# A hybrid encoder block: the last additions of v as accumulating stores, and the small work of q and k in groups of four

## The chip, the cores and the metric

The kernel runs on one core of one Trainium2 chip. The metric is device microseconds for one execution of the whole program; lower is better. The core has a matrix engine (PE), a vector engine (DVE), a scalar engine (ACT) and a general engine (POOL); SP only issues DMAs here. Each engine takes its instructions strictly in its own program order, and semaphores hold an instruction until what it reads is there and what it overwrites has been read. Times inside the execution are counted from the start of the profiled span.

## The reference

The input has 512 tokens of 1024 channels. One normalised input feeds three token mixers (a pooling mixer, a linear recurrence and an attention) and their gates; the outputs are merged and projected, and a SwiGLU network follows. What the change touches is this, cut from the reference:

```python
# linear recurrence (width 1024)
log_a = (-LRU_C * r) * softplus(-lru_lambda)
a = exp(log_a)
b = sqrt(-expm1(2.0 * log_a)) * (i * xc)
_, h = lax.associative_scan(combine, (a, b), axis=1)      # h[s] = a[s] * h[s-1] + b[s]

# attention: q, k, v are 512 x 1024 each, cut from h @ w_in, as 8 heads of 128
q = rms_norm(q, q_norm)        # over the 128 channels of a head
k = rms_norm(k, k_norm)
y = stick_breaking_attention(q, k, v)
```

So q and k need, per token and head, the sum of 128 squares and a scaling by its inverse root; v is used as the projection leaves it.

## The kernel before

**Matmuls in three passes.** Every large product in float32 is done as three passes of a rounded type: high part of the data by high part of the weight, high by low, low by high. `split_w` (L134 to L143) makes the parts of each weight tile of 128x1024: ACT copies the raw tile into `whi` (L141), DVE subtracts it from the raw tile into `wlo` (L142). In the program order of PE the second matmul of a tile is the first that reads `wlo`. The tiles come from a pool with three buffers of each kind, so the parts of one tile may be written once PE is through with the tile three places earlier.

**Products of v, k and q.** The three projections run one after the other in the order v, k, q (t = 2, 1, 0). Each is a two by two block product done with seven products instead of eight (`ORDER`: 11, 12, S2, S1, S3, S4, 22), and each of the seven is two weight tiles of 12 matmuls (`tok_product`, L836). The weights of S2, S1, S3 and S4 are sums of the four loaded blocks: `qs` (L214) and the second form of `qw` (L209) are such sums on DVE, and others are built by DMAs that add while they load (POOL, L200 and L215). This text numbers the tiles as the program does: `wlo24` to `wlo37` belong to v, 38 to 51 to k, 52 to 65 to q. A *block* is one tile's 12 matmuls.

**Quarters of the result.** Each projection has four quarters, (0,0), (0,1), (1,0), (1,1). A quarter is the sum of two PSUM tiles that are ready at different times: `snap` copies the first to SBUF as `r` (ACT, L857), and `final` adds the second to it (DVE, L865, 128x1024). For v, `post` then stores `r` to `qd` in DRAM (POOL, L790). For k it takes squares with row sums (ACT, eight small instructions, L803), forms the inverse root on POOL and DVE, scales (ACT, eight small instructions, L823), transposes (DVE, L814) and stores; for q the scaling is applied later.

**The recurrence runs beside v.** Its four channel chunks end in passes of DVE over 128x1024: `lru_decay` (L703), `lru_input` (L711 and L712), two scans of 128x512 (`lru_scan`, L717), then `lru_store`, which copies to a high part `yh` on ACT (L722), subtracts on DVE (L723) and stores both (POOL, L725). Chunks 2 and 3 are still open when v begins.

**What sets the order.** Small pieces of work lie in a list, `bg`, and `tick()` takes one from it, once before and once after the matmuls of each tile. Above that a scheduler of the build sorts by priority: `high_priority` moves an instruction ahead, and `issue_after(x)` keeps instructions behind x in the order. `issue_after` decides the order alone and adds no wait on the chip. All weight loads are issued on SP's queue; adding loads and stores lie on POOL's.

Of the kernel before, what the change touches and what calls it, by code (L numbers as in the profile page):

```python
# [64 lines left out]
def layer_kernel(ctx: ExitStack, tc: tile.TileContext, x, xt, vecs, w_in, w_qkv7, w_gate7, w_pool, w_rg, w_ig,  # L65
# [65 lines left out]

    los, raws = [], []

    def split_w(raw, shape, n):  # L134
        hi, lo = weight_tiles("whi" + n, "wlo" + n)
        if len(shape) == 3:
            hi, lo = (t.rearrange("p (a b) -> p a b", a=shape[1]) for t in (hi, lo))
        else:
            hi, lo = (t.rearrange("p (a b c) -> p a b c", a=shape[1], b=shape[2]) for t in (hi, lo))
        with tc.high_priority(60):  # L140
            act(hi, raw, AF.Copy)  # L141
            los.append(dve.tensor_tensor(lo, raw, hi.bitcast(F32), ALU.subtract).ins)  # L142
        return hi, lo  # L143
# [47 lines left out]
    def seven_load(n, nms):  # L191
# [3 lines left out]
        for nm in nms:  # L195
            for i in range(pieces):
                qraw[u, nm, i] = r = b4(list(shape), f"qw{u}{nm}{i}", "w")
                nc.sync.dma_start(r, seven_src(u, nm, i))
                if nm == "21":
                    nc.gpsimd.dma_start(r, seven_src(u, "22", i), accum_op=ALU.add)  # L200

    def add_seven(un, nm, i):
        u, pieces, shape = UNITS[un]
        last = i == pieces - 1

        def make(n):
            if nm == "S4":
                r = qraw[u, "12", i]
                dve.tensor_tensor(r, r, qraw[u, "S2", i], ALU.add)  # L209
            src = qraw[u, {"S1": "21", "S3": "11", "S4": "12"}.get(nm, nm), i]  # L210
            parts = split_w(src, [P] + list(shape), n)
            if nm == "11":
                qraw[u, "S2", i] = r = b4(list(shape), f"qs{u}{i}")
                dve.tensor_tensor(r, qraw[u, "21", i], src, ALU.add)  # L214
                add = nc.gpsimd.dma_start(src, seven_src(u, "21", i), accum_op=ALU.add)  # L215
            if last:
# [220 lines left out]
    with ExitStack() as first:  # L437
# [322 lines left out]
        def of(f, c):  # L760
            return lambda: f(c)
# [17 lines left out]
        gate1(2)  # L779
        for f, c in ((lru_decay, 2), (lru_decay, 3), (lru_input, 2)):  # L780
            step(of(f, c))
# [11 lines left out]
        def post(t, i, j, r):  # L793
            if t == 2:
                store(t, i, j, r)
                return
            z = b4([2, 512], f"sq{t}{i}{j}")
            sums = qss[:, 2 * j:2 * j + 2, 4 * i:4 * i + 4] if t == 0 else cst.tile(
                [P, 2, 4], F32, tag="ssq", name=f"ssq{t}{i}{j}", bufs=2)
            for a in range(2):  # L800
                for n in range(4):
                    cs = slice(n * HD, (n + 1) * HD)
                    act(z[:, a, cs], r[:, a, cs], AF.Square, accum_out=sums[:, a, n:n + 1])  # L803
            if t == 0 and i > j:
                state["last"] = lambda: turn(t, i, j, r, z)
                return
            if t == 0:
                turn(t, i, j, r, z)
                return
            dve.tensor_scalar(sums, sums, 1.0 / HD, EPS, ALU.mult, ALU.add)  # L810
            bg.append(lambda: post2(t, i, j, r, z, sums))

# [4 lines left out]
        def post2(t, i, j, r, z, s_):  # L817
            y = cst.tile([P, 2, 4], F32, tag="krs", name=f"krs{i}{j}", bufs=2)
            rsqrt(y, s_, (2, 4), f"q{t}{i}{j}")
            for a in range(2):  # L820
                for n in range(4):
                    v = r[:, a, n * HD:(n + 1) * HD]
                    act(v, v, AF.Copy, scale=y[:, a, n:n + 1])  # L823
            turn(t, i, j, r, z)

# [23 lines left out]
        for t in VKQ:  # L849
# [4 lines left out]
            def snap(key, src):  # L854
                r[key] = b4([2, 512], f"r{t}{key[0]}{key[1]}")
                with tc.high_priority(EARLY):
                    state["snap"] = act(two(r[key]), in_order(src), AF.Copy, scale=-1.0 if key[0] else 1.0)  # L857
# [5 lines left out]
            def final(key, src):  # L863
                v = two(r[key])
                dve.tensor_tensor(v, v, in_order(src), ALU.subtract if key[0] else ALU.add)  # L865
# [9 lines left out]
            for nm in ORDER:  # L875
# [928 lines left out]
```

## Time and profile before

| | |
|---|---|
| three runs, median | 860.64 us (859.68 to 860.79) |
| the profiled execution | 858.89 us |
| its span, first to last instruction | 856.8 us |
| PE busy | 850.3 us (99% of the span) |
| DVE, ACT, POOL busy | 732.3, 533.3, 88.6 us |
| granted TensorE clock | 1.00 throughout |

The gates before v end near 138 us of the span; v takes the stretch from there to about 176 us, k to about 213, and q to about 249. In the groups and timelines, `out<-in` gives the tiles that an instruction writes and reads, and the bracket at the end of a row tells how long the engine stood still before it, and what ended that. Matmuls overlap in the pipeline, so their rows of 0.38 us start 0.216 us apart when nothing is waited for, and a larger step between two starts is a stall.

### The profile page before, as it was taken

How to read it: one execution, taken by the hardware profiler on the slowest of the kernel's cores; microseconds unless marked ns; L12 is line 12 of the kernel's file. 1: busy time of each engine (PE TensorE's matmuls, PEld its weight loads, DVE VectorE, ACT ScalarE, POOL GpSimd, SP SyncE). 2: the span in 40 equal slices, each digit the busy share in tenths (PEclk: the TensorE clock that was granted, in tenths of full speed). 3: DMA queues.
4: the chain of work that ended last, by engine and by line, in shares of the span. 5: the costliest groups of instructions: out<-in, count | busy, mean ns of one | idle time of the engine just before them, and what ended most of it. 6: DMA issues, size and time to landing. Idle time of an engine off the chain costs nothing.

```text
span 856.8 us, 14307 instructions
## 1 busy us (share of the span) xinstructions
PE 850.3 (99%) x5483; PEld 781.2 (91%) x5483; DVE 732.3 (85%) x937; ACT 533.3 (62%) x863; POOL 88.6 (10%) x128
## 2 busy tenths in 40 slices
PE   9999999999999999999999999999999999999998
PEld 7888888888889988889889988889999999999998
DVE  7899898987897699967997877799988888999974
ACT  6554999658887657556665544455655555755642
POOL 1110002123324102000001100000000000121200
PEclk9999999999999999999999999999999999999999
DMA  9586356798585768846668854364533434797913
GB/s 343 160 286 205 101 167 200 215 316 262 141 257 129 228 170 239 246 116 171 174 204 212 182 197 148 99 164 136 145 99 109 114 101 142 221 238 204 199 32 123
DMA packets 141988, 154.09 MB, mean 180 GB/s; under 512 B 41696, under 2 KB 115424, under 8 KB 141920
## 3 DMA queue, kind: packets, MB, share of 16 engines
q1 hardware_dynamic: 129248, 107.30, 40.6%
q0 software_dynamic: 12528, 45.62, 22.5%
q8 instruction: 43, 0.70, 0.3%
q10 hardware_dynamic: 144, 0.26, 0.1%
q14 instruction: 25, 0.20, 0.1%
HBM read 132.71 MB, written 18.87 MB: 177 GB/s over the span
## 4 chain that ended last, share of the span: by engine, by line
PE 88%; ACT 4%; DVE 4%; issue 3%; POOL 1%; DMA 0%; DVEq 0%; POOLq 0%
PE ps_y L315 11%; PE ps_x L315 8%; PE ps_dy L1723 6%; PE ps_q L844 5%; PE ps_dx L1723 5%; PE ps_br L306 3%; PE ps_br L307 3%; PE ps_br L308 3%; PE ps_bY L1347 3%; PE ps_gy L315 3%; PE ps_gate L736 2%; PE ps_bX L1347 2%; PE ps_gx L315 2%; PE ps_pool L308 2%; PE ps_pool L306 2%
## 5 line engine op out<-in xcount | busy, mean ns | idle before, releaser
L141 ACT ACTIVATE whi<-raw 128x1024 fp32r<-128x1024 f32 x69 | 72.9, 1056 | 75.6 <-PE ps_br L307 18.4
L142 DVE TENSOR_TENSOR wlo<-raw,whi 128x1024 fp32r<-128x1024 f32 x69 | 84.2, 1220 | 22.4 <-ACT whi L141 21.9
L142 DVE TENSOR_TENSOR wlo<-qw,whi 128x1024 fp32r<-128x1024 f32 x48 | 58.3, 1220 | 11.6 <-ACT whi L141 11.2
L141 ACT ACTIVATE whi<-qw 128x1024 fp32r<-128x1024 f32 x48 | 50.4, 1052 | 23.6 <-PE ps_q L844 12.8
L1508 ACT ACTIVATE wh_S<-w_S 128x1024 fp32r<-128x1024 f32 x36 | 38.3, 1063 | 28.7 <-PE ps_y L315 20.0
L1629 POOL DMA_DIRECT2D dw<-in_w_down_dram x20 | 17.0, 855 | 305.3 <-DMA dw<-in_w_down_dram 247.7
L1509 DVE TENSOR_TENSOR wl_S<-w_S,wh_S 128x1024 fp32r<-128x1024 f32 x36 | 43.8, 1220 | 3.3 <-ACT wh_S L1508 3.3
L1508 ACT ACTIVATE wh<-w 128x1024 fp32r<-128x1024 f32 x27 | 28.6, 1061 | 28.0 <-PE ps_x L315 9.4
L1509 DVE TENSOR_TENSOR wl<-w,wh 128x1024 fp32r<-128x1024 f32 x27 | 32.9, 1220 | 8.2 <-ACT wh L1508 8.2
L1508 ACT ACTIVATE whdS<-dw 128x1024 fp32r<-128x1024 f32 x20 | 21.2, 1061 | 20.7 <-PE ps_dy L1723 10.6
L1155 DVE TENSOR_TENSOR_SCAN E<-K,ahead 128x512 f32<-128x512 f32 (+3 forms) x32 | 25.4, 814 | 4.6 <-ACT K L1151 4.6
L1509 DVE TENSOR_TENSOR wldS<-dw,whdS 128x1024 fp32r<-128x1024 f32 x20 | 24.3, 1221 | 5.2 <-ACT whdS L1508 5.2
L306 PE MATMUL ps_lru<-HH,whi 128*128 128x512 f32 x64 | 24.6, 384 | 0.0
L306 PE MATMUL ps_br<-yph,whi 128*128 128x512 f32 x64 | 24.4, 382 | 0.0
L306 PE MATMUL ps_gate<-HH,whi 128*128 128x512 f32 x64 | 24.4, 381 | 0.0
L307 PE MATMUL ps_br<-ypl,whi 128*128 128x512 f32 x64 | 24.3, 380 | 0.0
L306 PE MATMUL ps_pool<-HH,whi 128*128 128x512 f32 x64 | 24.3, 379 | 0.0
L306 PE MATMUL ps_br<-yHH,whi 128*128 128x512 f32 x64 | 24.3, 379 | 0.0
L307 PE MATMUL ps_lru<-HL,whi 128*128 128x512 f32 x64 | 24.3, 379 | 0.0
L308 PE MATMUL ps_lru<-HH,wlo 128*128 128x512 f32 x64 | 24.3, 379 | 0.0
L307 PE MATMUL ps_gate<-HL,whi 128*128 128x512 f32 x64 | 24.3, 379 | 0.0
L308 PE MATMUL ps_gate<-HH,wlo 128*128 128x512 f32 x64 | 24.3, 379 | 0.0
(742 smaller groups left out, 3432.1 us busy)
## 6 DMA issues: line engine op xcount, KB each, us to landing
raw<-in_w_in_dram SPq DMA_DIRECT2D x31, 512.0 KB, 5.1
qw<-in_w_qkv_dram SPq DMA_DIRECT2D x24, 512.0 KB, 7.2
dw<-in_w_down_dram POOLq DMA_DIRECT2D x20, 512.0 KB, 7.7
w<-in_w_ffn_gate_dram SPq DMA_DIRECT2D x36, 256.0 KB, 3.9
w<-in_w_ffn_up_dram SPq DMA_DIRECT2D x36, 256.0 KB, 4.1
raw<-in_w_branch_dram SPq DMA_DIRECT2D x16, 512.0 KB, 3.8
qw<-in_w_qkv_dram POOLq DMA_DIRECT2D x12, 512.0 KB, 7.6
g<-gd SPq DMA_DIRECT2D x24, 256.0 KB, 4.5
```

The costliest lines, as they stand in the source:

```text
L141: act(hi, raw, AF.Copy)
L142: los.append(dve.tensor_tensor(lo, raw, hi.bitcast(F32), ALU.subtract).ins)
L306: nc.tensor.matmul(ps, lh, rh, start=start, stop=False, skip_group_check=skip)
L307: nc.tensor.matmul(ps, lh, rl, start=False, stop=False, skip_group_check=skip)
L308: nc.tensor.matmul(ps, ll, rh, start=False, stop=stop, skip_group_check=skip)
L315: nc.tensor.matmul(o, a_[a][:, w, k, :], il2(b_[b][:, k, :]), start=first and n == k == 0, stop=last and n == 2 and k == 3, skip_group_che ...
L844: nc.tensor.matmul(ps[:, a, :], b_[:, k, ts_], il(a_[:, kk, :]), start=first and n == k == 0, stop=n == 2 and k == 3, skip_group_check=True)
L1155: dve.tensor_tensor_scan(E[:, c0:c0 + n][:, ::-1], K[:, c0 + 1:c0 + n + 1][:, ::-1], ahead[:, S - n:][:, ::-1], 0.0, ALU.mult, ALU.add)
L1347: nc.tensor.matmul(o, ah[x_][:, w, k, :], il2(b[k][y_]), start=first_ and n == k == 0, stop=n == 2 and k == 3, skip_group_check=True)
L1508: act(h, src, AF.Copy)
L1509: dve.tensor_tensor(l, src, h.bitcast(F32), ALU.subtract)
L1723: nc.tensor.matmul(o, a_[a][:, w, k0 + k, :], il2(b_[b][:, k, :]), start=first and i == k == 0, stop=last and i == 2 and k == nk - 1, skip ...
```

## The change

**v.** `snap` stores its copy `r` to `qd` at once. The second PSUM tile of a quarter is copied to SBUF by ACT (`add_store`, a tile `v`), and a DMA on POOL's queue with an adding write puts it on top of what is in `qd`. The four additions L865 of v leave DVE; four copies on ACT and four stores of 512 KB come in. An adding store waits for the landing of the plain store to the same rows.

**The recurrence.** The high part `yh` of chunks 0 and 1 is made on DVE instead of ACT, and the second half of `lru_decay` of chunks 2 and 3 too. The passes L711, L712 and L717 of chunks 2 and 3, the sums `qs` and the additions L209 of v's weights stand behind named low parts (`seven_lo`).

**q and k.** The eight squares and the eight scalings of a quarter are issued as two groups of four, each placed behind the newest `whi`, with two ticks between the groups.

Nothing is changed in the order of PE or of SP. DVE has one row fewer, ACT one fewer, POOL four more. Lines behind L199 move down by 7, those of the end by 34.

```diff
@@ split_w
-    los, raws = [], []
+    his, los, raws = [], [], []
...
-            act(hi, raw, AF.Copy)
+            his.append(act(hi, raw, AF.Copy).ins)
@@ add_seven
+    seven_lo = {}
...
-                dve.tensor_tensor(r, r, qraw[u, "S2", i], ALU.add)
+                with tc.issue_after(seven_lo["S2", i]) if un == 0 else nullcontext():
+                    dve.tensor_tensor(r, r, qraw[u, "S2", i], ALU.add)
...
-            if nm == "11":
+            if un == 0:
+                seven_lo[nm, i] = los[-1]
+            if nm == ("12" if un == 0 else "11"):
+                first_ = qraw[u, "11", i]
                 qraw[u, "S2", i] = r = b4(list(shape), f"qs{u}{i}")
-                dve.tensor_tensor(r, qraw[u, "21", i], src, ALU.add)
-                add = nc.gpsimd.dma_start(src, seven_src(u, "21", i), accum_op=ALU.add)
+                with tc.issue_after(los[-1]) if un == 0 else nullcontext():
+                    dve.tensor_tensor(r, qraw[u, "21", i], first_, ALU.add)
+                add = nc.gpsimd.dma_start(first_, seven_src(u, "21", i), accum_op=ALU.add)
@@ lru_decay, lru_store
-            if c < 2:
-                dve.tensor_scalar(t, t, -1.0, 1.0, ALU.mult, ALU.add)
-            else:
-                act(t, t, AF.Identity, scale=-1.0, bias=1.0)
+            dve.tensor_scalar(t, t, -1.0, 1.0, ALU.mult, ALU.add)
...
-            act(h, y, AF.Copy)
+            if c < 2:
+                dve.tensor_copy(h, y)
+            else:
+                act(h, y, AF.Copy)
@@ post (k, q)
-            for a in range(2):
-                for n in range(4):
-                    cs = slice(n * HD, (n + 1) * HD)
-                    act(z[:, a, cs], r[:, a, cs], AF.Square, accum_out=sums[:, a, n:n + 1])
+            def squares(a):
+                with nullcontext() if t == 0 and i > j else behind_hi():
+                    for n in range(4):
+                        cs = slice(n * HD, (n + 1) * HD)
+                        act(z[:, a, cs], r[:, a, cs], AF.Square, accum_out=sums[:, a, n:n + 1])
...
+            squares(0)
...
+                bg.extend([nothing, nothing, then])
+        def behind_hi():
+            return tc.issue_after(his[-1])
@@ post2 (k)
+            scale(0)
+            bg.extend([nothing, nothing, lambda: (scale(1), turn(t, i, j, r, z))])
@@ the loop over v, k, q
+                if t == 2:
+                    store(t, *key, r[key])
...
+            def add_store(key, src):
+                part = b4([2, 512], f"v{key[0]}{key[1]}")
+                with tc.high_priority(EARLY):
+                    act(two(part), in_order(src), AF.Copy, scale=-1.0 if key[0] else 1.0)
+                nc.gpsimd.dma_start(rows(t, *key), part, accum_op=ALU.add)
...
             def final(key, src):
+                if t == 2:
+                    add_store(key, src)
+                    return
...
+                if t == VKQ[0]:
+                    for f, after_ in {"11": ((lambda: lru_input(2), ("12", 0)), (lambda: lru_input(3), ("12", 1))),
+                                      "12": ((lambda: lru_scan(2, 0), ("S2", 0)), (lambda: lru_scan(2, 1), ("S2", 1))),
+                                      "S2": ((lambda: lru_scan(3, 0), ("S1", 0)), (lambda: lru_scan(3, 1), ("S1", 1)))
+                                      }.get(nm, ()):
+                        with tc.issue_after(seven_lo[after_]):
+                            f()
                 if (t, nm) == (VKQ[0], "S3"):
-                    def last_scan():
-                        for j in range(2):
-                            with tc.issue_after(los[j - 5]):
-                                lru_scan(3, j)
-
-                    step(of(lru_input, 3)), step(of(lru_scan, 2)), step(last_scan)
                     step(of(lru_store, 2)), step(of(lru_store, 3))
```

On DVE, at the start of v, the order before around the low parts of the third, fourth and fifth tile (`wlo_1341` is wlo26, `wlo_1368` is wlo27, `wlo_1395` is wlo28; `qs`, `qw` are sums of v's weights; `lt`, `ls`, `li` belong to the recurrence):

```order
L214 TENSOR_TENSOR qs_1262<-qw_1194,qw_1200 128x1024
L214 TENSOR_TENSOR qs_1302<-qw_1197,qw_1202 128x1024
L703 SCALAR_TENSOR_TENSOR lt_1224<-lr_1082,lt_1224 128x1024
L142 TENSOR_TENSOR wlo_1341<-qw_1204,whi_1340 128x1024
L711 SCALAR_TENSOR_TENSOR ls_1249<-lr_897,ls_1249 128x1024
L209 TENSOR_TENSOR qw_1204<-qw_1204,qs_1262 128x1024
L142 TENSOR_TENSOR wlo_1368<-qw_1206,whi_1367 128x1024
L712 TENSOR_TENSOR ls_1249<-ls_1249,li_898 128x1024
L142 TENSOR_TENSOR wlo_1395<-qs_1262,whi_1394 128x1024
```

and now, where `wlo_1333` is wlo26, `wlo_1363` wlo27 and `wlo_1398` wlo28:

```order
L142 TENSOR_TENSOR wlo_1294<-qw_1202,whi_1293 128x1024
L711 TENSOR_SCALAR lt_1118<-lt_1118 128x1024
L711 TENSOR_SCALAR lt_1224<-lt_1224 128x1024
L142 TENSOR_TENSOR wlo_1333<-qw_1204,whi_1332 128x1024
L221 TENSOR_TENSOR qs_1336<-qw_1194,qw_1200 128x1024
L715 SCALAR_TENSOR_TENSOR ls_1249<-lr_897,ls_1249 128x1024
L142 TENSOR_TENSOR wlo_1363<-qw_1206,whi_1362 128x1024
L221 TENSOR_TENSOR qs_1366<-qw_1197,qw_1202 128x1024
L142 TENSOR_TENSOR wlo_1398<-qs_1336,whi_1397 128x1024
```

The two sums `qs` stood ahead of wlo26, and now stand behind wlo26 and wlo27; the addition to `qw` and the pass L712 that stood around wlo27 have moved further back.

On DVE, later in v, the order before from wlo31 (`wlo_1445`) to wlo35 (`wlo_1526`):

```order
L142 TENSOR_TENSOR wlo_1445<-qw_1197,whi_1444 128x1024
L712 TENSOR_TENSOR ls_1251<-ls_1251,li_1083 128x1024
L717 SCALAR_TENSOR_TENSOR li_898<-lt_1118,ls_1249 128x512
L142 TENSOR_TENSOR wlo_1470<-qw_1200,whi_1469 128x1024
L142 TENSOR_TENSOR wlo_1486<-qw_1202,whi_1485 128x1024
L717 SCALAR_TENSOR_TENSOR li_1083<-lt_1224,ls_1251 128x512
L142 TENSOR_TENSOR wlo_1509<-qw_1204,whi_1508 128x1024
L717 SCALAR_TENSOR_TENSOR li_1083<-lt_1224,ls_1251 128x512
L142 TENSOR_TENSOR wlo_1526<-qw_1206,whi_1525 128x1024
```

and now, from wlo31 (`wlo_1451`) to wlo36 (`wlo_1562`):

```order
L142 TENSOR_TENSOR wlo_1451<-qw_1197,whi_1450 128x1024
L716 TENSOR_TENSOR ls_1251<-ls_1251,li_1083 128x1024
L721 SCALAR_TENSOR_TENSOR li_898<-lt_1118,ls_1249 128x512
L142 TENSOR_TENSOR wlo_1479<-qw_1200,whi_1478 128x1024
L721 SCALAR_TENSOR_TENSOR li_1083<-lt_1224,ls_1251 128x512 x2
L142 TENSOR_TENSOR wlo_1495<-qw_1202,whi_1494 128x1024
L142 TENSOR_TENSOR wlo_1519<-qw_1204,whi_1518 128x1024
L142 TENSOR_TENSOR wlo_1536<-qw_1206,whi_1535 128x1024
L142 TENSOR_TENSOR wlo_1562<-qw_1208,whi_1561 128x1024
```

wlo33 (`wlo_1486` before) stood right behind wlo32; now both scans of the last chunk (one row, x2) stand between wlo32 and wlo33 (`wlo_1495`), and none behind it.

On POOL, the DMAs from the middle of the gates' stores (`gd`) to the stores of the recurrence, before (`qd` are the results in DRAM, `qw` the adding loads; `qw_1448` and `qw_1451` are blocks 21 of k):

```order
L215 DMA qw_1200<-in_w_qkv_dram 128x1024
L215 DMA qw_1202<-in_w_qkv_dram 128x1024
L603 DMA gd_96<-gt_1253 128x2x512
L603 DMA gd_97<-gt_1335 128x2x512
L790 DMA qd_88<-r_1391 128x2x512
L200 DMA qw_1448<-in_w_qkv_dram 128x1024
L200 DMA qw_1451<-in_w_qkv_dram 128x1024
L790 DMA qd_89<-r_1505 128x2x512
L725 DMA ydh_103<-yh_1585 128x1024
L725 DMA ydl_105<-li_898 128x1024
```

and now, where `v` are the new adding stores and `qw_1454` and `qw_1457` the same blocks of k:

```order
L610 DMA gd_96<-gt_1253 128x2x512
L610 DMA gd_97<-gt_1327 128x2x512
L222 DMA qw_1200<-in_w_qkv_dram 128x1024
L222 DMA qw_1202<-in_w_qkv_dram 128x1024
L797 DMA qd_88<-r_1389 128x2x512
L891 DMA qd_88<-v_1429 128x2x512
L200 DMA qw_1454<-in_w_qkv_dram 128x1024
L797 DMA qd_88<-r_1472 128x2x512
L200 DMA qw_1457<-in_w_qkv_dram 128x1024
L797 DMA qd_89<-r_1514 128x2x512
L891 DMA qd_89<-v_1555 128x2x512
L797 DMA qd_89<-r_1558 128x2x512
```

The adding loads of v have gone behind the stores of gates, the adding store of (0,0) stands ahead of the first block of k, a plain store ahead of the second, and the adding store of (1,1) ahead of the store of (1,0) and of all that follows on the queue, the stores of chunks 2 and 3 of the recurrence first.

More of the change, by code (lines that the diff above doesn't have):

```diff
@@ L779, in layer_kernel @@
         gate1(2)
-        for f, c in ((lru_decay, 2), (lru_decay, 3), (lru_input, 2)):
+        for f, c in ((lru_decay, 2), (lru_decay, 3)):
             step(of(f, c))
@@ L793, in post @@
         def post(t, i, j, r):
-            if t == 2:
-                store(t, i, j, r)
-                return
             z = b4([2, 512], f"sq{t}{i}{j}")
@@ L799, in post, with then @@
                 [P, 2, 4], F32, tag="ssq", name=f"ssq{t}{i}{j}", bufs=2)
-            for a in range(2):
-                for n in range(4):
-                    cs = slice(n * HD, (n + 1) * HD)
-                    act(z[:, a, cs], r[:, a, cs], AF.Square, accum_out=sums[:, a, n:n + 1])
-            if t == 0 and i > j:
[L805 to L811, printed above, removed]
+            def squares(a):
[3 more added lines that the diff above has]
+                        act(z[:, a, cs], r[:, a, cs], AF.Square, accum_out=sums[:, a, n:n + 1])
+            def then():
+                squares(1)
+                if t == 0 and i > j:
+                    state["last"] = lambda: turn(t, i, j, r, z)
+                    return
+                if t == 0:
+                    turn(t, i, j, r, z)
+                    return
+                dve.tensor_scalar(sums, sums, 1.0 / HD, EPS, ALU.mult, ALU.add)
+                bg.append(lambda: post2(t, i, j, r, z, sums))
+            squares(0)
+            if t == 0 and i > j:
+                then()
+            else:
+                bg.extend([nothing, nothing, then])
+        def behind_hi():
+            return tc.issue_after(his[-1])
         def turn(t, i, j, r, z):
@@ L819, in post2, with scale @@
             rsqrt(y, s_, (2, 4), f"q{t}{i}{j}")
[L820 to L824, printed above, removed]
+            def scale(a):
+                with behind_hi():
+                    for n in range(4):
+                        v = r[:, a, n * HD:(n + 1) * HD]
+                        act(v, v, AF.Copy, scale=y[:, a, n:n + 1])
+            scale(0)
+            bg.extend([nothing, nothing, lambda: (scale(1), turn(t, i, j, r, z))])
         def q_scales():
```

1 line of the change is left out of this document (added).

## Prediction

> **What bounds the kernel now.** I read the page's first part, then the waits of PE, then the busy time by windows over v, k and q, then PE and DVE in order of time around each stall.
>
> ```profile
> span 856.8 us, 14307 instructions
> PE 850.3 (99%) x5483; PEld 781.2 (91%) x5483; DVE 732.3 (85%) x937; ACT 533.3 (62%) x863; POOL 88.6 (10%) x128
> ...
> PE ps_q L844 <- DVE wlo L142: 1.5, 4, 0.5
> PE ps_q0S L844 <- DVE wlo L142: 0.2, 1, 0.2
> ...
> 140.00:150.00 10.00, 9.16 (x41) 7.39 (x41) 10.00 (x10) 9.16 (x12) 3.27 (x4) 1.00 0.79 180
> 150.00:160.00 10.00, 10.00 (x48) 8.74 (x48) 10.00 (x10) 5.14 (x5) 1.45 (x2) 1.00 0.53 179
> 160.00:170.00 10.00, 9.64 (x45) 8.13 (x44) 9.10 (x9) 6.40 (x7) 1.88 (x4) 1.00 0.94 229
> 170.00:180.00 10.00, 10.00 (x48) 8.77 (x47) 10.00 (x10) 5.45 (x6) 4.64 (x7) 1.00 1.07 408
> 220.00:230.00 10.00, 9.71 (x45) 8.20 (x44) 8.87 (x10) 10.00 (x25) 1.20 (x2) 1.00 0.22 68
> 230.00:240.00 10.00, 9.78 (x45) 8.12 (x44) 6.00 (x9) 8.01 (x21) 3.71 (x4) 1.00 0.98 302
> ```
>
> PE is the bound. The change leaves PE's order alone, so it can only win what PE stands still in v, k and q, and by the two rows of waits that is 1.7 us, all of it for a `wlo` of DVE. The windows (columns: PE, PEld, DVE, ACT, POOL, clock, DMA share, GB/s) put it at 140 to 150, 160 to 170 and in q at 220 to 240; windows without a stall hold 10.00. The missing PE time of the four windows is 0.84 + 0.36 + 0.29 + 0.22 = 1.71 us. In v DVE is full (10.00), so there a low part is late because of what stands before it on DVE.
>
> The starts of the matmuls give the full price of a stall:
>
> ```profile
> 140.69 0.38 PE L844 MATMUL ps_q<-whi,HH 128*128 128x512 f32 x1
> 140.90 0.38 PE L844 MATMUL ps_q<-wlo,HH 128*128 128x512 f32 x1
> ...
> 143.28 0.38 PE L844 MATMUL ps_q<-whi,HH 128*128 128x512 f32 x1
> 143.95 0.48 PE L844 MATMUL ps_q<-wlo,HH 128*128 128x512 f32 x1 [0.29 <-DVE wlo L142]
> 144.27 0.38 PE L844 MATMUL ps_q<-whi,HL 128*128 128x512 f32 x1
> ...
> 146.43 0.38 PE L844 MATMUL ps_q<-whi,HH 128*128 128x512 f32 x1
> 147.35 0.48 PE L844 MATMUL ps_q<-wlo,HH 128*128 128x512 f32 x1 [0.55 <-DVE wlo L142]
> ...
> 160.19 0.38 PE L844 MATMUL ps_q<-whi,hT3h 128*128 128x512 f32 x1
> 160.93 0.48 PE L844 MATMUL ps_q<-wlo,hT3h 128*128 128x512 f32 x1 [0.36 <-DVE wlo L142]
> ```
>
> An undisturbed block takes 143.28 − 140.69 = 2.59 us, and its second matmul starts 0.216 after the first (a twelfth of that). At wlo26 the step is 0.67 and the next one 0.32, so it loses 0.45 + 0.10 = 0.56 us; wlo27 loses 0.70 + 0.10 = 0.81 and wlo32 0.52 + 0.10 = 0.63. That is 2.0 us in v. That is 2.0 us in v, where the windows miss 0.84 + 0.36 = 1.2; in the same ratio q's 0.51 are 0.85. So some 2.9 us, 0.33% of the time, is the most that this change can win.
>
> **Part 1, DVE in v.** The low parts now stand elsewhere, and I go through DVE's new order with the durations of the old:
>
> ```profile
> 142.68 1.22 DVE L142 TENSOR_TENSOR wlo<-qw,whi 128x1024 fp32r<-128x1024 f32 x1
> 143.81 1.22 DVE L711 SCALAR_TENSOR_TENSOR ls<-lr,ls 128x1024 f32<-128x1024 f32 x1
> 146.08 1.22 DVE L142 TENSOR_TENSOR wlo<-qw,whi 128x1024 fp32r<-128x1024 f32 x1
> ...
> 151.76 1.21 DVE L865 TENSOR_TENSOR r<-r,ps_q 128x1024 f32<-128x1024 f32 x1
> ...
> 161.93 1.22 DVE L717 TENSOR_TENSOR_SCAN li<-lt,ls 128x512 f32<-128x512 f32 x1
> ...
> 140.76 1.05 ACT L141 ACTIVATE whi<-qw 128x1024 fp32r<-128x1024 f32 x1
> ...
> L649 DVE CAST xch<-xc 128x1024 fp32r<-128x1024 f32 x1 | 0.7, 683 | 0.0
> ```
>
> Each of these operations, additions and scans too, starts 1.13 us after the one before and ends 1.22 after its start. PE wants wlo26 at 143.28 + 0.216 = 143.49, and each later one 2.59 us on: wlo27 at 146.08, wlo28 148.67, wlo32 159.03, wlo33 161.62.
>
> - From wlo25 to wlo26 stood two sums `qs` and a pass, 3 x 1.13 us; now there are two passes that read one tile, for which the nearest row is the CAST of 0.68 us. wlo26 is then bound by its `whi`. That one ran on ACT from 140.76 to 141.8; ACT loses two such copies ahead of it, `yh` of chunks 0 and 1, and behind it the two passes L707. I bring it forward by 1.3 of the 2.1, to end at 140.5. So wlo26 runs from 140.5 to 141.7, ahead of 143.49: its stall of 0.56 goes. Behind it stand one `qs`, one pass and wlo27, which ends at 140.5 + 3 x 1.13 + 1.22 = 145.1, 0.96 us before PE wants it: the stall of 0.81 goes too.
> - What moved back is late next. From wlo27 to wlo33 the new order holds 16 operations back to back, 16 x 1.128 = 18.05 us, while PE takes 6 blocks, 15.53 us. With the 0.96 in hand wlo33 is 18.05 − 15.53 − 0.96 = 1.56 us late. On the way wlo31 ends at 156.38, wanted at 156.44, just in time; wlo32 ends at 159.76, 0.73 late. So PE stalls twice, at wlo32 and at wlo33, by 1.56 in all and 0.1 each for the restart: 1.7 us.
> - The additions L865 of v, 4 x 1.13 us, leave DVE. Only one of the four, at 151.76, lies ahead of the last stall, and it is already out of the count above. The others lay behind wlo33, where DVE has no hurry: nothing won.
>
> v loses 1.7 us instead of 2.0: **−0.3 us**. The bounds come from the time of wlo26: a microsecond earlier, and wlo33 alone is 0.56 late, v loses 0.7, −1.3; half a microsecond later, and wlo31 to wlo33 stall by 2.06 and three restarts, v loses 2.4, +0.4.
>
> **Part 2, the four copies on ACT.** They take the place of DVE's additions, about 1.0 us each. ACT has room in v, 5.14 and 6.40 of 10 in the windows from 150, and it waits for PE with 1.5 us at a time:
>
> ```profile
> 155.21 1.06 ACT L141 ACTIVATE whi<-qw 128x1024 fp32r<-128x1024 f32 x1 [1.53 <-PE ps_q L844]
> 156.18 1.00 ACT L857 ACTIVATE r<-ps_q 128x1024 f32<-128x1024 f32 x1
> ```
>
> A copy of 1.0 in a gap of 1.53 costs nothing; were it put ahead of a `whi` without the gap, wlo would come up to 1.0 later, which the 1.13 of DVE's own queue hides but for wlo32 and wlo33. I take 0.
>
> **Part 3, the four adding stores and POOL's queue.** No store with addition is in the trace. The nearest rows are the adding loads:
>
> ```profile
> q0 software_dynamic: 2302, 8.39, 62.4%
> ...
> qw<-in_w_qkv_dram POOLq DMA_DIRECT2D x6, 512.0 KB, 7.7
> qd<-r POOLq DMA_DIRECT2D x4, 512.0 KB, 8.0
> ...
> 161.89 0.87 POOL L200 DMA_DIRECT2D qw<-in_w_qkv_dram  x1 [1.67 <-DMA qw<-in_w_qkv_dram]
> ...
> DMA to landing us min/median/max: 5.6/7.5/9.5
> ...
> 171.96 1.22 DVE L214 TENSOR_TENSOR qs<-qw,qw 128x1024 f32<-128x1024 f32 x1
> 173.10 1.22 DVE L142 TENSOR_TENSOR wlo<-qw,whi 128x1024 fp32r<-128x1024 f32 x1
> 174.23 1.22 DVE L214 TENSOR_TENSOR qs<-qw,qw 128x1024 f32<-128x1024 f32 x1
> ```
>
> From 140 to 190, POOL's queue (columns: packets, MB, share) used 62.4% of 50 us, 31 us of all engines, for 8.39 MB, 16 DMAs of 512 KB. At the 408 GB/s of the window 170 to 180 a plain one takes 1.3 us; ten of them 13, which leaves 3.0 us for each of the six adding ones (my estimate). So each adding store takes 1.3 to 3.0 us of all engines, in a stretch where the DMA share is 0.94 and 1.07 already. No one reads `qd` of v before q is done, so its own landing hurts nobody. What hurts is what comes later through it: the blocks 21 of k. The second was issued at 161.89 and landed 9.5 us later (the longest of the row), at 171.4, and `qs` for k reads it on DVE. Before, that `qs` (174.23) stood behind wlo38; now both `qs` stand ahead of wlo38 on DVE, so whoever waits for the block holds wlo38, and PE behind that. PE wants wlo38 at 143.49 + 12 x 2.59 + 1.7 of stalls = 176.3; it must start by 175.1, and the second `qs` by 173.9. Ahead of this block on the queue there are now an adding store and a plain store more: landing at 171.4 + 1.3 = 172.7 at best, 171.4 + 1.3 + 3.0 = 175.7 at worst, which costs 0 to 1.8 us. The plain store is certain, the adding one is issued about 153 and mostly done by then (the window 150 to 160 has 0.53 of DMA): I take the near end, **0**, and keep +1.8. There is no gain on the other side, since PE waits for nothing in k.
>
> The Trainium skill ("DMA: Bandwidth & Descriptors", sections "Issuing engines are not separate DMA queues" and "Rules for kernel authors") says that DMAs from whatever engine share the same 16 hardware engines, and that an adding DMA must wait for an earlier one to the same bytes. The trace agrees with the first: the same 512 KB of q0 take from 5.6 to 9.5 us to land as the windows fill. It speaks against the change; by it, what the stores take from the loads is the 1.3 to 3.0 above.
>
> The second wait is at POOL's issue: the adding store of (1,1) waits for a plain store to land (8.0 in the middle), and holds the stores of the recurrence and two adding loads of k (`qw_1498`, `qw_1500`) behind it. They are issued about 2 us later than before; k needs them ten blocks into k, about 195. Cost 0.
>
> **Part 4, k and q.** In k PE has no stall, and ACT and DVE keep their sums, so I cost it at 0; the cover is PE's own full queue, and without it a group of four squares ahead of a `whi` would cost 4 x 0.30 = 1.2 us. In q the stall at wlo56 came from ACT:
>
> ```profile
> 222.37 1.23 DVE L142 TENSOR_TENSOR wlo<-qs,whi 128x1024 fp32r<-128x1024 f32 x1 [1.13 <-ACT whi L141]
> ...
> L803 ACT ACTIVATE sq<-r 128x128 f32<-128x128 f32 x56 | 16.5, 298 | 2.5 <-DVE r L865 2.5
> L814 DVE STREAM_TRANSPOSE sq<-r 128x1024 f32<-128x1024 f32 x7 | 8.7, 1242 | 0.5 <-ACT r L823 0.5
> ```
>
> wlo56 ended at 223.60, some 0.4 late (0.29 missing in the window, and the restart). The scalings now come earlier, but the transposition (1.24) now stands ahead of wlo56 and fills the 1.13 that DVE had waited: wlo56 ends 0.1 earlier at most. The stall at wlo62 hangs on the same chain as before. **−0.1 us**, with bounds −0.9 (all of q's stalls go) and +1.2 (the transposition late by its own length).
>
> **Sum.** −0.3 + 0 + 0 − 0.1 = −0.4 us on the profiled 858.89, 858.5. The median of the runs is 1.75 above the profiled execution, so I forecast 860.64 − 0.4 = 860.2.
>
> **Rivals.** The measurement tells 0.2%, 1.7 us, from no change.
>
> - *The stalls of v are gone, not moved.* The additions were the burden, DVE has 4.5 us less to do, and wlo32 and wlo33 come in time. For it: DVE is the only engine named. Against it: three of the four additions lie behind the last stall, and both scans now lie ahead of wlo33. It gives −2.0, with q up to −2.9: 858.6 to 857.7, middle 858.2. Chance 0.17.
> - *Slower: the adding stores delay the blocks of k.* Place: the second `qs` ahead of wlo38; it decides from a landing later than 173.9. Its price by the upper bound is +1.8, and if the adding stores cost twice an adding load (a read, and a write to DRAM), 3.0 more, +4.8; less 0.4. That is 862.0 to 865.0, middle 863.0. For it: DMA at 1.07, and DVE's in-order queue. Against it: the room of two microseconds, and the adding store that starts early. Chance 0.18.
> - *The change does not do what it says*: the stalls only change their tiles, and what q wins v loses. 0 ± 0.3, 860.6. It lies within my forecast's own bounds.
>
> **How the numbers follow.** Forecast (with the last rival) 0.65, first rival 0.17, slower rival 0.18. The forecast's own range is 859.2 to 861.6. The first rival is faster by over 1.7 us in most of its range, the second slower in most of it; a little of the forecast's mass goes past either side and replaces what they leave: faster 0.17, same 0.66, slower 0.17. The range reaches to 858.4 and to 862.4, which leaves a tenth on either side.
>
> **What would show it.** Right: PE's starts step evenly at wlo26 and wlo27, and stall at wlo32 and wlo33 by 0.7 to 0.9 each; DVE 10.00 from 145 to 164; k without a wait of PE; q with two stalls as before. Wrong: no wait for `wlo` in v (first rival); a wait of PE for wlo38 with DVE idle before `qs` for a DMA `qw` (slower rival); or waits of ACT for `qw` in k.

## The result, and the profile after

The change makes the kernel slower: 861.82 us (median of 22 runs, 858.22 to 864.70) against 859.30 us before (22 runs beside them, 858.16 to 860.98). The ratio is 1.003, with a 95% interval of 1.0022 to 1.0037, some 2.5 us.

The first profiled execution of the changed kernel took 859.09 us, near the lowest of its 22 runs, and so shows v as changed and nearly nothing of the loss. From its page, its waits of PE, and PE and DVE in order of time in v:

```profile
span 857.2 us, 14317 instructions
PE 850.2 (99%) x5483; PEld 781.8 (91%) x5483; DVE 730.7 (85%) x937; ACT 533.0 (62%) x863; POOL 93.4 (11%) x132
...
PE ps_q L866 <- DVE wlo L142: 1.4, 3, 0.5
PE ps_br L314 <- DMA yHL<-ydl: 0.7, 1, 0.7
PE ps_q0S L866 <- DVE wlo L142: 0.2, 1, 0.2
...
139.96 1.23 DVE L142 TENSOR_TENSOR wlo<-qw,whi 128x1024 fp32r<-128x1024 f32 x1 [0.72 <-ACT whi L141]
143.37 1.22 DVE L142 TENSOR_TENSOR wlo<-qw,whi 128x1024 fp32r<-128x1024 f32 x1
...
159.36 0.48 PE L866 MATMUL ps_q<-wlo,hT3h 128*128 128x512 f32 x1 [0.53 <-DVE wlo L142]
162.73 0.48 PE L866 MATMUL ps_q<-wlo,hT3h 128*128 128x512 f32 x1 [0.51 <-DVE wlo L142]
...
DMA to landing us min/median/max: 8.0/8.0/8.0
```

v is as forecast: wlo26 (139.96) and wlo27 (143.37) are early and their stalls are gone, and PE now waits for wlo32 and wlo33. DVE and ACT have as many instructions as before (937 and 863), and DVE is busy for 1.6 us less. What is not as forecast begins at the last row, the first adding load for q (block 21): 8.0 us from its issue at 197.03 to its landing at 205.06. Before, it was issued at 193.75 and landed 5.6 us later (the shorter of the two loads in that view):

```profile
193.75 0.91 POOL L200 DMA_DIRECT2D qw<-in_w_qkv_dram  x1
...
DMA to landing us min/median/max: 5.6/7.1/8.6
```

A second trace of the changed kernel is of an execution of 863.37 us, in the upper part of the runs, and shows where that one loses. Waits of PE, PE in order of time, DVE in order of time, and windows:

```profile
PE ps_q L866 <- DVE wlo L142: 3.6, 4, 1.9
...
209.19 0.38 PE L866 MATMUL ps_q<-whi,hT4h 128*128 128x512 f32 x1
211.50 0.48 PE L866 MATMUL ps_q<-wlo,hT4h 128*128 128x512 f32 x1 [1.94 <-DVE wlo L142]
211.82 0.38 PE L866 MATMUL ps_q<-whi,hT4l 128*128 128x512 f32 x1
212.04 0.49 PE L866 MATMUL ps_q<-whi,hT4h 128*128 128x512 f32 x1
212.32 0.63 PE L866 MATMUL ps_q<-wlo,hT4h 128*128 128x512 f32 x1
212.75 0.63 PE L866 MATMUL ps_q<-whi,hT4l 128*128 128x512 f32 x1
...
215.66 0.38 PE L866 MATMUL ps_q<-whi,HH 128*128 128x512 f32 x1
...
202.76 1.22 DVE L142 TENSOR_TENSOR wlo<-qw,whi 128x1024 fp32r<-128x1024 f32 x1
209.09 1.22 DVE L221 TENSOR_TENSOR qs<-qw,qw 128x1024 f32<-128x1024 f32 x1 [5.11 <-DMA qw<-in_w_qkv_dram]
210.23 1.22 DVE L142 TENSOR_TENSOR wlo<-qw,whi 128x1024 fp32r<-128x1024 f32 x1
...
212.00:216.00 4.00, 4.00 (x12) 3.20 (x12) 4.00 (x5) 3.34 (x18) 1.86 (x2) 0.57 0.80 273
```

DVE stands still for 5.11 us before a sum `qs` of q's weights, because the adding load that it reads has not landed. wlo51, the last low part of k, stands behind this sum. PE starts the second matmul of the block 2.31 us after the first instead of 0.216: 2.1 us lost, and 0.1 at the restart. Then a second loss follows: the matmuls from 212.04 to 215.66 start up to 0.427 us apart, twice the usual step, and the granted clock of that window is 0.57. Nine matmuls take 3.62 us instead of 1.94, 1.7 us more. Together 3.9 us.

Not every execution loses in this way. The granted clock, averaged over the execution, is 0.998 in 4 of the 28 runs of this kernel (863.37 to 864.66 us), where 4 us at 0.57 would put it, and 0.999 or 1.00 in the others, among them runs of 863.98, 864.05 and 864.70 us. No execution near the median was traced. That the adding stores cause the excess of the median is shown by the runs below; at which stalls a usual execution loses it is not shown.

### The profile page after: what moved, and what is told of

Its sections match the earlier page's. It is cut to its first block, busy times and chain, and to the rows that moved or that the text cites. A ratio compares the mean times of both kernels' runs of the same rounds, so it can differ in the third digit from the quotient of the medians.

```text
span 857.2 us, 14317 instructions
## 1 busy us (share of the span) xinstructions
PE 850.2 (99%) x5483; PEld 781.8 (91%) x5483; DVE 730.7 (85%) x937; ACT 533.0 (62%) x863; POOL 93.4 (11%) x132
## 4 chain that ended last, share of the span: by engine, by line
PE 76%; issue 8%; DVE 5%; ACT 5%; DMA 4%; POOL 2%; SPq 0%; POOLq 0%; ACTq 0%; DVEq 0%
PE ps_y L322 11%; PE ps_x L322 8%; PE ps_dy L1757 6%; PE ps_dx L1757 5%; PE ps_br L314 3%; PE ps_br L315 3%; PE ps_br L313 3%; PE ps_q L866 3%; PE ps_bY L1381 3%; PE ps_gate L743 2%; PE ps_gy L322 2%; DVE wlo L142 2%; PE ps_bX L1381 2%; DMA qw<-in_w_qkv_dram 2%; PE ps_gx L322 2%
## 5 line engine op out<-in xcount | busy, mean ns | idle before, releaser
L314 PE MATMUL ps_br<-yHL,whi 128*128 128x512 f32 x64 | 24.4, 381 | 0.7 <-DMA yHL<-ydl 0.7
L315 PE MATMUL ps_br<-yHH,wlo 128*128 128x512 f32 x64 | 24.3, 380 | 0.0
L315 PE MATMUL ps_br<-yph,wlo 128*128 128x512 f32 x64 | 24.3, 380 | 0.0
```

Source lines behind the costliest of these rows:

```text
L314: nc.tensor.matmul(ps, lh, rl, start=False, stop=False, skip_group_check=skip)
L315: nc.tensor.matmul(ps, ll, rh, start=False, stop=stop, skip_group_check=skip)
```

## The experiments

Ratios are to the kernel before, run beside on the same chip. *Before* had 859.84 us beside the first four, 859.77 beside the next four, and 859.94 beside the three after those.

**The changed kernel again.**

> The changed kernel once more, unaltered, to see whether its excess over the kernel before (861.82 against 859.30, +2.5 us in the median) is there again and in which stage it lies; its first profiled execution was a fast one (859.09) and shows only +0.95 us at one late reload of the recurrence (yHL) beside v -0.2 and q +0.2. Both theories: +2 to +3 us. Theory A (adding stores and what they do to DMA timing): the trace shows a PE wait whose last link is a DMA. Theory B (groups of four in k and q): a PE wait for wlo or whi between 176 and 249.

862.78 us, ratio 1.0034 (1.0022 to 1.0046). This is the second trace above. It has a PE wait for a `wlo` between 176 and 249, as theory B expected, but that `wlo` waits for a DMA through DVE, as theory A did. The next three runs decide between them.

**Without the adding stores.** v's additions go back to DVE, everything else stays.

```diff
             def snap(key, src):
 ...
-                if t == 2:
-                    store(t, *key, r[key])
             def final(key, src):
-                if t == 2:
-                    add_store(key, src)
-                    return
                 v = two(r[key])
                 dve.tensor_tensor(v, v, in_order(src), ALU.subtract if key[0] else ALU.add)
 ...
+                elif t == 2:
+                    bg.append(lambda key=key, v=r[key]: store(2, *key, v))
```

> The changed kernel with v's four additions back on DVE and one plain store per quarter; the rest of the change is kept. Theory A (adding stores cost the time): the excess goes, ratio to before 0.998 to 1.001, that is -1.5 to +0.8 us, where v's own stalls may be up to 1 us longer since DVE has the additions again. Theory B (groups): +2 to +3 us stay.

858.43 us, ratio 0.9985 (0.9977 to 0.9994). The excess is gone, and the rest of the change wins 1.3 us here. In its trace the adding loads for q land 5.2 and 8.7 us after their issue, and PE has no wait at wlo51:

```profile
PE ps_q2S L866 <- DVE wlo L142: 0.5, 1, 0.5
PE ps_q0S L866 <- DVE wlo L142: 0.2, 1, 0.2
PE ps_q L866 <- DVE wlo L142: 0.2, 1, 0.2
...
DMA to landing us min/median/max: 5.2/6.9/8.7
```

PE's waits for `wlo` add up to 0.9 us, less than the 1.6 of the changed kernel. In the new order, taking the additions off DVE did not help v: from v's first matmul to the first one of k's product S1 (block 44, the first that writes `ps_q1S`) it takes 53.27 us here, 53.58 with the adding stores, 53.81 before.

**The adding stores alone**, put into the kernel before:

```diff
             def final(key, src):
+                if t == 2:
+                    add_store(key, src)
+                    return
```

> The kernel before with nothing but the adding stores in v (four additions off DVE, four ACT copies, four more DMAs). Theory A: +2 to +4 us. Theory B: -1 to +0.3 us, since the one addition ahead of wlo30 leaves DVE.

863.73 us, ratio 1.0047 (1.0035 to 1.0059), +3.9 us. The same place and the same two losses, PE's wait for wlo51 behind DVE's wait for the adding load, and the slow matmuls. A third one is at wlo38, the first of k (first row of PE):

```profile
  DVE qs L214: 5.1, 1
...
DMA to landing us min/median/max: 12.6/13.0/13.5
...
175.93 0.48 PE L844 MATMUL ps_q<-wlo,HH 128*128 128x512 f32 x1 [0.45 <-DVE wlo L142]
...
211.80 0.48 PE L844 MATMUL ps_q<-wlo,hT4h 128*128 128x512 f32 x1 [1.93 <-DVE wlo L142]
```

At wlo38 PE loses 0.7 us: DVE waited 1.22 us for the second adding load of k, which landed at 173.50. In return the stall at wlo32, 0.63 us before, is not there. All five runs have a granted clock of 0.997 or 0.998.

**Without the groups of four.** `post` and `post2` of the kernel before, all else as changed.

> The changed kernel with the squares and scalings of q and k issued as before, eight at a time; v and the recurrence as changed. Theory A: +2 to +3 us as the changed kernel. Theory B: -0.5 to +0.5 us.

860.49 us, ratio 1.0015 (1.0001 to 1.0029), between the two theories, its runs spread from 858.12 to 864.34. In its trace the first adding load for q landed at 207.12, late enough for DVE to wait 3.00 us, but PE lost only 0.1 at wlo51: the kernel runs at the edge of the stall. Behind this, PE loses 0.4 and 0.2 us at wlo54 and wlo55, where before has no stall, and 1.0 at wlo56, where before loses 0.6. The intervals of this kernel and of the changed one overlap, so whether the groups bear on the loss stays open.

What in the adding stores does it? In the trace of 863.37 us, POOL's queue in order of time, then the time to landing of the stores issued at 181.75 and 183.30 and of the adding load issued at 196.52:

```profile
162.94 1.04 POOL L797 DMA_DIRECT2D qd<-r  x1
175.66 1.21 POOL L891 DMA_DIRECT2D qd<-v  x1 [11.69 <-issue]
...
181.75 1.20 POOL L891 DMA_DIRECT2D qd<-v  x1
183.30 1.20 POOL L891 DMA_DIRECT2D qd<-v  x1 [0.34 <-issue]
...
196.52 0.92 POOL L200 DMA_DIRECT2D qw<-in_w_qkv_dram  x1 [3.62 <-DMA qw<-in_w_qkv_dram]
...
DMA to landing us min/median/max: 18.6/18.6/18.6
...
DMA to landing us min/median/max: 22.0/22.0/22.0
...
DMA to landing us min/median/max: 12.5/12.5/12.5
```

Two things can be read. POOL issued nothing for 11.69 us ahead of the adding store of (1,1), which waits for the plain store issued at 162.94 (a wait for a DMA's landing that the row calls issue; the store landed 12.2 us after its issue, at 175.2). And the queue's transfers land one after another: the two last stores at 200.4 and 205.3, 4.9 us apart, and the adding load for q at 209.1, 3.8 us behind them. Theory W takes the first for the cause, theory Q the second. The issue of this load is 2.8 us later than before too, since POOL stands 3.62 us for the plain load into the same tile.

**The second store plain**, over the same rows, with the same wait, so that only the adding is gone (the kernel then leaves out one of v's two summands):

```diff
-                nc.gpsimd.dma_start(rows(t, *key), part, accum_op=ALU.add)
+                nc.gpsimd.dma_start(rows(t, *key), part)
```

> The changed kernel, but the second store of each quarter of v is a plain one over the same rows: it waits for the first one's landing as before and does not add (so v lacks one of its two summands). Theory Q (queue: an adding store holds POOL's queue for 4.4 to 4.9 us where a plain one takes 1.3, so the first adding load for q lands near 209 instead of 199 and the sum qs, ahead of wlo51 on DVE, comes late): three stores give back 3 x 3.3 = 10 us of the queue, wlo51 is in time, 858 to 859.5 us, -1 us against before. Theory W (wait: the store of (1,1) holds everything behind it on POOL for 10 to 12 us): the wait is still there, +2 to +3 us stay.

859.35 us, ratio 0.9993 (0.9984 to 1.0001): the excess goes, though the wait is kept (11.34 us). The same two stores, issued at 178.96 (14.2 us to landing) and 180.52 (15.2), and the adding load, issued at 195.63:

```profile
174.07 0.73 POOL L891 DMA_DIRECT2D qd<-v  x1 [11.34 <-issue]
...
DMA to landing us min/median/max: 14.2/14.7/15.2
...
DMA to landing us min/median/max: 9.2/9.2/9.2
```

The last store lands at 195.7 instead of 205.3, and the adding load at 204.8 instead of 209.1; DVE waits 0.87 us, and PE not at all at wlo51. The load was issued as the last store landed, with no transfer ahead of it on its queue, and still took 9.2 us where it took 5.6 before; why is not shown.

**No one waits behind the adding store.** Three of the adding stores are issued behind k's adding loads:

```diff
+                if key == (0, 0):
                     nc.gpsimd.dma_start(rows(t, *key), part, accum_op=ALU.add)
+                else:
+                    held.append((key, part))
 ...
+                if (t, nm) == (1, "11"):
+                    for key, part in held:
+                        with tc.issue_after(adds[1]):
+                            nc.gpsimd.dma_start(rows(2, *key), part, accum_op=ALU.add)
```

> The changed kernel with the adding stores of (1,1), (0,1) and (1,0) issued together behind k's two adding loads on POOL's queue, so that nothing of k or of the recurrence waits behind the store of (1,1). Theory W: the excess goes, 858 to 859.5 us. Theory Q: the three adding stores still lie ahead of the adding loads for q (landing near 205 to 209), +1 to +3 us stay.

859.43 us, ratio 0.9999 (0.9990 to 1.0007). This takes the excess away too, against theory Q. The wait of 11.69 us is gone, and the adding load for q lands at 205.7 (issued at 196.72, 9.0 us):

```profile
DMA to landing us min/median/max: 9.0/9.0/9.0
...
205.76 1.23 DVE L221 TENSOR_TENSOR qs<-qw,qw 128x1024 f32<-128x1024 f32 x1 [0.91 <-DMA qw<-in_w_qkv_dram]
```

DVE waits 0.91 us, and PE not at wlo51. (This trace is of an execution of 861.10 us; it also loses behind q, at steps of 1.09 near 349 and of 0.73 and 0.59 between 494 and 500.)

So each theory is half right: the excess over the kernel before needs both, stores that add and a queue that waits. (Against the kernel without adding stores 0.1 to 1.2 us may be left, which the intervals do not tell.) How far each pushes the load back, single traces do not tell. With one of the two it landed at 204.8 and 205.7; with both it landed at 205.1, 206.7, 207.1, 209.1 and 209.4 in the five traces that have them ahead of it, so it is late in some executions and not in others. The bound of the sum follows from the unstalled start of block 51 (209.19 in the trace of 863.37): wlo51 has to end at 209.4, and with it and the sum, 1.14 + 1.22 us, the sum must start by 207.0. The observed landings 204.8, 205.1, 205.7 (no stall at wlo51), 207.1 (0.1 us), 209.1 and 209.4 (2.1 us each) fit.

**The adding stores behind the loads for q.** As in the experiment above, but behind q's blocks 21 on the queue.

> The changed kernel with the same three adding stores issued behind the two adding loads for q (blocks 21). Theory Q: these loads land as before (199 and 204), no stall at wlo51, 857.8 to 859.3 us; what is late next are the adding loads of q's S3 blocks, some 10 us before they are needed. Theory W: the same, since the wait goes too. It shows whether anything of the adding stores costs time once they are out of the way; if buffers of v held 20 us longer stop ACT's copies in k, +1 us or more.

860.27 us, ratio 1.0015 (1.0000 to 1.0029). As expected the adding loads land 5.8 and 8.7 us after their issue, and wlo51 is in time. But 4 of its 12 runs took 863 to 865 us, with a granted clock of 0.996 to 0.998, and its trace (863.26) shows another loss far behind: in the last stage ACT waits 6.82 us for a load of the down projection's weights, and PE loses 3.9 us around it. Waits of PE, ACT and PE in order of time, and a window:

```profile
PE ps_dx L1765 <- ACT whd L1550: 0.9, 1, 0.9
PE ps_dx L1765 <- DVE wld L1551: 0.8, 1, 0.8
...
781.71 1.06 ACT L1550 ACTIVATE whd<-dr 128x1024 fp32r<-128x1024 f32 x1 [6.82 <-DMA dr<-in_w_down_dram]
...
782.82 0.38 PE L1765 MATMUL ps_dx<-Bd120h,whd 128*128 128x256 f32 x1 [0.93 <-ACT whd L1550]
...
784.08 0.53 PE L1765 MATMUL ps_dx<-Bd120h,wld 128*128 128x256 f32 x1 [0.77 <-DVE wld L1551]
...
785.00:790.00 5.00, 5.00 (x36) 5.00 (x35) 5.00 (x8) 3.32 (x5) 0.40 (x1) 0.74 0.62 211
```

These matmuls of 128x256 usually start 0.111 us apart. The two stalls are steps of 1.21 and 1.05 us with two matmuls between them, and behind them, from 784.41 to 787.40, the steps are 0.213 us, some 1.6 us of the loss with the restart. So slow matmuls follow here two stalls that are each shorter than the single one at wlo51.

Why this load is late in some executions of this one kernel was not tried; it stays open.

**The sum of q further back**, behind wlo54 and wlo55:

```diff
-            if nm == ("12" if un == 0 else "11"):
+            if nm == ("11" if un == 1 or un > 2 else "12"):
 ...
-                with tc.issue_after(los[-1]) if un == 0 else nullcontext():
+                with tc.issue_after(los[-1]) if un in (0, 2) else nullcontext():
```

> The changed kernel with the two sums qs of q placed behind wlo54 and wlo55 (as those of v are) instead of ahead of wlo51; adding stores unchanged. Both theories: the adding load for q still lands near 205 to 209, but DVE reaches wlo51 without waiting for it, so the PE stall at wlo51 and the slow matmuls behind it go: 858 to 860 us. If the stall only moves to wlo52 or wlo56, 861 or more.

861.78 us, ratio 1.0028 (1.0020 to 1.0037). The stall at wlo51 is gone, as expected, but in the trace others have come in q, and v, k and q together take 1.4 us longer than in the trace of before. POOL now issues q's next adding loads 8 us later, since they must wait for these sums, and an inverse root of k is formed at 225.84 instead of 214.26, behind these loads on POOL and behind its operand from DVE. The scalings of k on ACT come late and stand ahead of a `whi`:

```profile
233.98 1.23 DVE L142 TENSOR_TENSOR wlo<-qw,whi 128x1024 fp32r<-128x1024 f32 x1 [2.52 <-ACT whi L141]
...
235.26 0.48 PE L866 MATMUL ps_q<-wlo,hT3h 128*128 128x512 f32 x1 [0.78 <-DVE wlo L142]
```

So moving the one sum that meets the late load first did not cure it here.

**Stalls made on purpose**, without adding stores: wlo40, wlo45 and wlo50 are written three or four times.

```diff
+            k = {"40": 3, "45": 3, "50": 4}.get(n, 0)
+            if k:
+                with tc.high_priority(600):
+                    for _ in range(k):
+                        los.append(dve.tensor_tensor(lo, raw, hi.bitcast(F32), ALU.subtract).ins)
```

> The changed kernel without adding stores, where the low parts wlo40, wlo45 and wlo50 are written three, three and four times over (same values), so that PE is made to wait at three places in k by amounts between 1 and 6 us, with no DMA late. If the slow matmuls behind the stall at wlo51 (eight steps of 0.427 instead of 0.216 us, granted clock 0.57) come from the length of the stall, they follow here after stalls of 2 us and more, and not after those below about 1.3. If they came from the late DMA or the place, none follow here.

871.92 us in a single run. PE in order of time around wlo40, and the windows around wlo40 and wlo45:

```profile
180.65 0.38 PE L872 MATMUL ps_q<-whi,HH 128*128 128x512 f32 x1
184.37 0.48 PE L872 MATMUL ps_q<-wlo,HH 128*128 128x512 f32 x1 [3.34 <-DVE wlo L146]
...
185.12 0.63 PE L872 MATMUL ps_q<-wlo,HH 128*128 128x512 f32 x1
...
188.52 0.39 PE L872 MATMUL ps_q<-whi,HH 128*128 128x512 f32 x1
...
185.00:190.00 5.00, 5.00 (x17) 4.09 (x16) 2.85 (x4) 1.06 (x1) 0.00 (x0) 0.66 0.57 220
200.00:205.00 5.00, 4.55 (x21) 4.01 (x22) 3.00 (x6) 3.16 (x9) 0.00 (x0) 1.00 0.85 211
```

Behind the stall of 3.34 us (a step of 3.72 between two starts) eight matmuls take twice the step, from 185.12 to 188.52, with no DMA late. Behind that at wlo45 (the wait row gives 1.2 us, a step of 1.56) the clock stays at 1.00. At wlo50 two stalls came one matmul apart, steps of 2.40 and 1.53, and eleven steps of 0.427 follow. So the slow matmuls need no late DMA: they follow from the stalls themselves. A stall of 1.2 us alone did not bring them, one of 1.9 did; where between them the bound lies was not tried, and the two short stalls of the last stage above show that stalls close together count too.

**Without stores and without groups, and the kernel without adding stores again.**

> The changed kernel without adding stores and with the squares and scalings of q and k issued as before: only the new order of v's sums and of the recurrence is left. From the stage times of the kernel without adding stores (v -0.5 us, k and q -0.2 us in one profiled execution each): -0.5 us against before, of which the groups have no part; if the groups carried the gain, 0 +- 0.4.

> The changed kernel without adding stores once more, beside the run before it: 0.9985 +- 0.0009 of before as the first time, that is 858.0 to 859.0 us; the difference to the run without groups is what the groups bring.

859.12 us, ratio 0.9991 (0.9982 to 1.0000), and 859.11 us, ratio 0.9992 (0.9983 to 1.0001). They are alike: without adding stores the groups of four bring nothing that can be measured, and the new order of v and of the recurrence brings what there is. The first time it was 1.3 us and this time 0.8, so by the ratios this version beats the changed kernel by 3.3 to 4.2 us, and the kernel before by about 1 us, at the edge of what the runs tell.

**The kernel before again.** In every trace of a changed kernel PE waits near 350 us for a reload of the recurrence, and in the first trace of before it doesn't.

> The kernel before, unaltered, for a second trace of it. Every trace of a changed kernel so far shows a stall of 0.4 to 1.5 us where the branch product waits for the reload yHL (near 350 us), with and without adding stores; the one trace of before (its time 858.89, at the low end of its runs) has none. If the stall varies from execution to execution whatever the kernel, it is seen here in an execution of 859.5 us or more. If it comes from the change, there is none here.

859.46 us, ratio 0.9998 (0.9987 to 1.0009). Its profiled execution took 858.79 us, not the slower one that the expectation asked for, and still shows a step of 0.49 us there, 0.27 us of loss. So the wait comes without the change too. The traces have it from 0 to 1.4 us; whether the change makes it longer is not settled by two traces of before.

## Why the prediction was wrong

The forecast was 860.2 us, 0.4 less than before; the result is 2.5 us more than before.

- **What bounds the kernel, and Part 1**, held. The two stalls at wlo26 and wlo27 went; those at wlo32 and wlo33 came, with 0.79 and 0.78 us by the steps between starts, and 0.2 at wlo31, where the forecast had "just in time". v lost 1.8 us (forecast 1.7), and became 0.23 us shorter (forecast 0.3).
- **Part 2** held: no `whi` of v was late for the four copies.
- **Part 3 is the step that failed**, in three places. The price: an adding store was to take 1.3 to 3.0 us of the queue, bounded by the adding loads; the two in the trace of 863.37 landed 4.9 us apart, and in all traces adding stores one behind the other landed 4.2 to 6.0 us apart. The reach: the text followed the queue to k's blocks, found "Cost 0", and went no further. That was right for k, but the next loads on the same queue are q's blocks 21, and they are the ones that came late. The wait at POOL's issue: it was counted as a delay of 2 us for what stands behind it, and not as a time in which the queue drains and after which everything comes at once, on top of the adding stores. The plain store waited for took 10.4 and 12.2 us to land in the two traces of the changed kernel (8.0 was assumed). Each half, taken away alone, takes the excess away.
- **Part 4**: k indeed had no stall of its own. In q the forecast was −0.1 us; by the first trace the stalls of q are 1.4 us, where before has 1.2. A small miss, and too small to be told in the runs.
- **The slower rival** had the mechanism: an adding load late, a sum `qs` that waits for it on DVE, a `wlo` behind it, PE idle. It had it at wlo38, one projection too early for the changed kernel (in the trace of the adding stores alone wlo38 is late too, by 0.7 us), and gave it a chance of 0.18. The price it named, 1.8 to 4.8 us less 0.4, holds the 3.9 of the trace and the 2.5 of the runs, but that is luck, since it was made of other parts: it had no term for the slow matmuls, which are 1.7 of the 3.9.
- **The first rival** (all stalls of v gone) fell: in the new order the stalls at wlo32 and wlo33 came as DVE's order sets them. Nor had DVE 4.5 us less to do, only 1.6 over the whole span. Without adding stores, with the four additions on DVE, v is even shorter (53.27 against 53.58 us). In the old order the load did count: there the adding stores alone took away the stall at wlo32.

## What to carry to other kernels

An operation that is moved from a full engine to a queue has to be followed along that queue until it has drained, here for 45 us, across k to the loads for q, to the first transfer that someone waits for; that its own result has time tells nothing. A DMA that waits for an earlier DMA's landing stops all that is queued behind it, and two such delays that are harmless alone can pass the point of a stall together. The price of a stall of PE can be more than its length: behind one of 1.9 us, and behind two of 0.9 and 0.8 close together, slow matmuls added some 1.7 us more.

## What the runs showed of the hardware

- Behind a PE stall the clock can drop. After steps between two starts of 2.31 us (2.1 us lost, in two traces) and of 3.72 us, eight or nine matmuls ran up to 0.427 us apart instead of 0.216, some 3.5 us of slow running and 1.7 us of loss; after single steps of 1.33, 1.56 and 1.66 us none did. After two steps of 1.21 and 1.05 us, two matmuls apart, fourteen ran 0.213 us apart instead of 0.111. The Trainium skill ("TensorE: Matmul & The Clock Gate", section "Why this matters for your kernels") advises against idle gaps of more than about 3 us, after which the clock falls to half. The rows agree with the half, 0.427 against 0.216, but here an idle time of 1.9 us was enough, and in one trace two of 0.93 and 0.77 us.
- On POOL's queue, an adding store of 512 KB to DRAM landed 4.9 us behind the adding store ahead of it (the trace of 863.37 us); the plain store in its place, over the same rows, landed 2.5 us behind the one ahead of it (178.96 + 14.2 and 180.52 + 15.2).
